# When the next block's weights are split at a change of block

## The chip, the cores and the metric

The kernel runs on one core of a Trainium2 chip. The metric is the device time of one execution in microseconds (us), taken as the median of several. Engines are named as in the profile: PE is TensorE (its weight loads are PEld), DVE is VectorE, ACT is ScalarE, POOL is GpSimd, SP is SyncE, which issues the weight loads.

## The reference, cut to what matters

A sequence of 256 tokens of width 1024 goes through three layers in fp32: one hybrid layer (attention and mLSTM side by side, then an MLP) and two layers of differential attention beside a convolution, each followed by a gated feed-forward part. Around each block stands the same frame:

```
x = x + rms_norm(mixed @ w_out, g_mix_post)        # first layer, "norm"
u = rms_norm(x, g_mlp_pre) @ w_up
x = x + rms_norm(relu(u)**2 @ w_down, g_mlp_post)
...
x = x + (1.0 + gate1) * mixed                      # two later layers, "gate"
h2 = rms_norm_2(x, norm2_g[l]) * (1.0 + scale2) + shift2
f_gate, f_up = jnp.split(h2 @ w_ffn_in[l], 2, axis=-1)
x = x + (1.0 + gate2) * ((jax.nn.silu(f_gate) * f_up) @ w_ffn_out[l])
```

So the last product of a block (w_out, w_down, w_ffn_out) is added to x, the sum is normed row by row, and the normed rows are multiplied by the first weights of the next block.

## The kernel before

**Weights.** All weights stream from HBM once, in pieces called halves here: 128 x 1024 fp32, 512 KB. SP loads each into one of eight buffers `raw` (L192). A half is then split into a high part `whi` on ACT (L202) and the rest `wlo = raw - whi`; three of four rests are made on POOL (L206), the fourth on DVE (L208). A product is three matmuls in the single-pass format: high by high, low by high, high by low. There are nine buffers each of whi and wlo (HB = 9), so a half can be split only when the matmuls of the ninth half before it are done; its raw buffer then takes the next load, in the fixed order of `plan`.

**Order.** The program is written out by hand: each engine runs its instructions in the order of emission. After every half that is used up, `done()` counts it and calls `tick()`, which lets background work go one step and calls `pump()`: it emits splits until nine are made ahead of those used up, or until `rot["cap"]`.

**The change of block.** There are two token blocks, 0 and 1, of 128 rows each. `r_tail` (L397) ends a block: the last halves, 5 (w_out) or 6 (w_down, w_ffn_out), which it has all in hand. It runs them for token block 0 in full, then for token block 1 half by half. While PE is on block 1, the rows of block 0 are finished: added to x, squared and summed (ACT L506, or ACT L553 and DVE L554 first for the norm), the root on POOL (L498, L499), scaled (DVE L511, ACT L512). Then they are turned: eight transposes on PE (L531) into four banks, a gain on DVE (L537) and ACT (L539), and the split into the next block's left operand `hT` (ACT L589, DVE L590). `drain_q(chain)` emits the turning of block 0, ahead of row half CHAIN = 3 of block 1, that is after three of five or six. `done()` stands behind every row half of block 1.

`a2_block` (L321) begins the next block with 6, 7 or 8 halves held (`hold`): it first emits splits until these are made, then runs all for token block 0, with the turning of block 1 put ahead of the last of them (EARLY = 1), and then for block 1. `r_tail` caps the splits at six of them; what is over, the seventh and the eighth, is split at the start of `a2_block`, behind the finishing of block 1 on ACT.

The five changes of block, by their place in the profile, are called first to fifth in this text:

| | from, to | tail halves | held | made before the tail | window, us |
|---|---|---|---|---|---|
| first (norm) | w_out, w_up | 5 | 6 | 1 to 4 | 142 to 163 |
| second (norm) | w_down, w_in of layer 0 | 6 | 8 | 1 to 3 | 333 to 358 |
| third (gate) | w_out, w_ffn_in of layer 0 | 5 | 7 | 1 to 4 | 509 to 528 |
| fourth (gate) | w_ffn_out, w_in of layer 1 | 6 | 8 | 1 to 3 | 702 to 723 |
| fifth (gate) | w_out, w_ffn_in of layer 1 | 5 | 7 | 1 to 4 | 875 to 896 |

At the end of the last block nothing is left to split.

Of the kernel before, what the change touches and what calls it, by code (L numbers as in the profile page):

```python
# [21 lines left out]
NL = 2  # L22
FF1 = 4096
# [7 lines left out]
CAP = 6  # L31
# [6 lines left out]
PRE1, PRE2 = 3, 2  # L38
UPC, GAC = (3, 1), (3, 2)
TAIL = 5  # L40
WARM = 7
EARLY, CHAIN, TWO = 1, 3, 0
SETUP, GATES = 2, 1
TAPS_AT = 2
LOADS = 3
# [12 lines left out]
def tile_hybrid_then_diff(ctx: ExitStack, tc: tile.TileContext, I, out: bass.AP):  # L58
# [121 lines left out]
    state = dict(dma=0, step=0, made=0, taken=0, done=0)  # L180
# [46 lines left out]
    def pump(most=99):  # L227
        while state["step"] < 2 * len(plan) and most > 0:
            most -= 1
            if plan[state["step"] // 2][2] != "a" and (  # L230
                    state["made"] >= min(state["done"] + HB - rot["slack"], rot["cap"])):
                break
            do_step()
# [26 lines left out]
    def done():  # L260
        state["done"] += 1
        tick()

    def tick():
        for d in list(delayed):
            d[0] -= 1
            if d[0] <= 0:
                delayed.remove(d)
                d[1]()
        step_gen(fills)  # L270
        step_gen(fills2)
        if not rot["busy"]:
            step_gen(folds)
        pump()
        for _ in range(rate["bg"]):
            step_gen(bg)

# [116 lines left out]
                mm_tok(acc[t][n], xT, k, t, w, 0, slice(n * 512, n * 512 + 512), start, stop)  # L394
        done()

    def r_tail(tag, srcs, acc, fin, cap, need=None, last=False):  # L397
        rot["slack"] = 0
        pump()
        ws = [take(tag) for _ in srcs]  # L400
        rot["cap"] = state["taken"] + cap
        def mm(t, n, i):
            mm_tok(acc[t][n], srcs[i][0], srcs[i][1], t, ws[i], 0, slice(n * 512, n * 512 + 512),
                   False, i == len(ws) - 1)

        g = fin(0)
        for n in range(2):
            for i in range(len(ws)):
                if need and n == 0:
                    step_gen(fills2)  # L410
                    need(srcs[i][1])
                mm(0, n, i)
            next(g, None)
        chain.append(g)
        rot["busy"] = True
        g = fin(1)
        ahead = range(len(ws) if last else TWO)
        for i in ahead:
            mm(1, 0, i)
        if last:  # L420
            next(g, None)
        for i in range(len(ws)):
            if i == CHAIN:
                drain_q(chain)
            for n in range(1 if i in ahead else 0, 2):
                mm(1, n, i)
            if i == len(ws) - 1:
                if not last:
                    next(g, None)
                next(g, None)  # L430
                pend.append(g)
            done()


    def small(dst, src):
# [135 lines left out]
    def fin(post, t, acc, grow, gc, bc):  # L571
        st = st_tile()
        made = []

        def xn_of():
            if not made:
                made.append(xn_tile())
            return made[0]

        yield from post(t, acc, grow, xn_of, st)  # L580
        scale_x(t, made[0], st)
        yield
        yield from pre_trans(t, made[0], hT, gc, bc)
# [222 lines left out]
    def mod(l, vec, j):  # L806
        assert (l, vec) in made
        return modc[:, l, vec, j:j + 1]
# [57 lines left out]
    def hid_tile():  # L866
        return ab_tile((128, 2, 2, 256), FR)

    def ffn(ng, pre, prefix, up, down_tag, fin, mid=None, last=False):
        hid = {}  # L870
        prefix(hid)
        for g in range(pre, LAG):
            hid[g] = up(g)
        acc = [[acc_tile() for _ in range(2)] for _ in range(2)]
        for g in range(LAG, ng):
            if mid and g == ng - 3:
                mid()
            hid[g] = up(g)
            if g == LAG:
                assert FDEL < 3  # L880
                drain_q(fills)
            h = hid.pop(g - LAG)
            for kk in range(2):
                r_half(down_tag, h, kk, acc, g == LAG and kk == 0, False)
        srcs = [(hid[g], kk) for g in range(ng - LAG, ng) for kk in range(2)]
        r_tail(down_tag, srcs, acc, lambda t: fin(t, acc[t]), CAP, last=last)

    def hid_from_tok(h, full, t):
        ps = ps_tile().rearrange("p (c t) -> p c t", c=4)
# [273 lines left out]
    for k in range(8 - TAIL):  # L1163
# [3 lines left out]
    hT = new_T()  # L1167
    mlp_c = (lambda j: gcol("g_mlp_pre", j), None)
    r_tail("out1", [(mixT, k) for k in range(8 - TAIL, 8)], acc,
           lambda t: fin(post_norm, t, acc[t], gmix, *mlp_c), CAP, need)  # L1170
    gmlp = row_tile(I["g_mlp_post"])

    def prefix1(hid):
# [33 lines left out]
    def to_layer(l, fin):  # L1207
        gc = lambda j: mod(l, 1, j)
        bc = lambda j: mod(l, 0, j)
        return lambda t, acc: fin(t, acc, gc, bc)  # L1210
# [4 lines left out]
            hT = new_T()  # L1215
        yield from fin(post_norm, t, acc, gmlp, gc, bc)

    ffn(FF1 // 256, PRE1, prefix1, up1, "down", to_layer(0, end_mlp))


    for l in range(NL):
# [191 lines left out]
        for k in range(8 - TAIL):  # L1413
# [1 line left out]
        hT = new_T()  # L1415

        r_tail("out2", [(mixT, k) for k in range(8 - TAIL, 8)], acc,
               lambda t: fin(post_gate, t, acc[t], g1, lambda j: mod(l, 4, j), lambda j: mod(l, 3, j)), CAP)
        gfin = row_tile(I["final_g_2"], name="vt") if l == NL - 1 else None
        g2 = []  # L1420

# [40 lines left out]
        def end_all(t, acc):  # L1462
# [7 lines left out]
            yield  # L1470

        ffn(FF2 // 256, PRE2, prefix2, up2, "fo", end_all if l == NL - 1 else to_layer(l + 1, end_layer),
            lambda: g2.append(gate_tile(l, 5)), l == NL - 1)


# [25 lines left out]
```

## Time and profile before

| | |
|---|---|
| median of 3 executions | 1084.35 us (1082.03 to 1085.1) |
| the profiled execution, its own time | 1083.16 us |
| its span, first to last instruction | 1081.4 us |
| PE busy | 1036.0 us, 96% |
| POOL, DVE, ACT busy | 691.5, 647.9, 558.8 us |
| mean granted TensorE clock | 0.985 |

PE is nearly always busy, so the time is PE's work and the few stretches in which it waits or runs at the lower of its two clocks. A row of the timeline below gives the start in us from the span's beginning, the time from start to end, the engine, the line, the operation, output and inputs, shapes, how many instructions were merged, and in brackets the idle time of the engine before it and what ended it.

### The profile page before, as it was taken

The numbers are of one execution on the slowest core, as the hardware profiler recorded it, in microseconds if no ns is written. First come the engines' busy times: TensorE is split into PE (matmuls) and PEld (weight loads), VectorE is DVE, ScalarE is ACT, GpSimd is POOL, SyncE is SP. The second block draws the span as 40 slices with busy tenths as digits, with TensorE's granted clock in tenths as the row PEclk, the third lists the DMA queues.
The fourth block names the chain that finished last, engine by engine and source line by source line (L and its number), as shares of the span: only waits on it lengthen the run. The fifth ranks groups of instructions, "written<-read, shape, count | busy, mean of one in ns | idle before, by whom it ended". The sixth has DMA issues, their size and how long they took to land.

```text
span 1081.4 us, 17255 instructions
## 1 busy us (share of the span) xinstructions
PE 1036.0 (96%) x6459; PEld 917.6 (85%) x6459; DVE 647.9 (60%) x1161; ACT 558.8 (52%) x933; POOL 691.5 (64%) x424
## 2 busy tenths in 40 slices
PE   8879989999998999989999999999999899999997
PEld 6667769899886789988798998888899778999995
DVE  4536556887854497834679797547873554441224
ACT  5745746444455556665643434475676545443441
POOL 2474648566575797846656665859967458566661
PEclk9989999999999999999999999999999999999999
DMA  8554545999974565546499999837635456765631
GB/s 259 169 176 130 192 146 189 345 356 362 329 268 136 167 185 165 187 156 175 132 353 318 332 343 358 299 104 214 186 127 175 137 175 224 258 224 180 198 108 39
DMA packets 169424, 231.84 MB, mean 214 GB/s; under 512 B 10215, under 2 KB 109757, under 8 KB 169339
## 3 DMA queue, kind: packets, MB, share of 16 engines
q1 hardware_dynamic: 169211, 230.71, 65.0%
q8 instruction: 51, 0.84, 0.3%
q14 instruction: 34, 0.28, 0.1%
q0 software_dynamic: 128, 0.02, 0.0%
HBM read 229.64 MB, written 1.06 MB: 213 GB/s over the span
## 4 chain that ended last, share of the span: by engine, by line
PE 75%; POOL 8%; DVE 6%; ACT 6%; issue 3%; DMA 2%; POOLq 0%; SPq 0%; DVEq 0%; ACTq 0%
PE bank L288 17%; PE bank L289 17%; PE bank L290 17%; PE bank L300 12%; POOL wlo L206 6%; PE bank L302 6%; ACT whi L202 2%; DVE bank L762 2%; DVE wlo L208 2%; DMA raw<-in_ada_w_dram 2%; PE bank L840 1%; ACT xn L506 1%; PE bank L860 1%; PE bank L531 1%; PE bank L832 0%
## 5 line engine op out<-in xcount | busy, mean ns | idle before, releaser
L206 POOL TENSOR_TENSOR wlo<-raw,whi 128x1024 fp32r<-128x1024 f32 x255 | 631.5, 2498 | 259.1 <-ACT whi L202 228.4
L202 ACT ACTIVATE whi<-raw 128x1024 fp32r<-128x1024 f32 x332 | 337.4, 1054 | 78.3 <-DMA raw<-in_w_down_dram 30.6
L288 PE MATMUL bank<-T,whi 128*128 128x256 f32 x1072 | 307.7, 287 | 2.3 <-DVE sc L773 2.3
L290 PE MATMUL bank<-T,wlo 128*128 128x256 f32 x1072 | 303.4, 283 | 0.0
L289 PE MATMUL bank<-T,whi 128*128 128x256 f32 x1072 | 303.3, 283 | 0.0
L288 PEld LDWEIGHTS bank<-T,whi 128*128 128x128 f32 x1072 | 205.1, 191 | 6.8 <-issue 3.7
L289 PEld LDWEIGHTS bank<-T,whi 128*128 128x128 f32 x1072 | 205.2, 191 | 1.1
L290 PEld LDWEIGHTS bank<-T,wlo 128*128 128x128 f32 x1072 | 205.1, 191 | 0.0
L300 PE MATMUL bank<-whi,T 128*128 128x512 f32 (+1 forms) x672 | 185.0, 398 | 7.3 <-ACT T L589 4.7
L208 DVE TENSOR_TENSOR wlo<-raw,whi 128x1024 fp32r<-128x1024 f32 x77 | 125.5, 1630 | 100.6 <-ACT whi L202 100.1
L300 PEld LDWEIGHTS bank<-whi,T 128*128 128x128 f32 x672 | 123.9, 192 | 36.6 <-ACT T L589 6.1
L762 DVE SCALAR_TENSOR_TENSOR bank<-raw,cact,bank 128x512 f32<-128x512 f32 x168 | 126.9, 755 | 7.5 <-DMA raw<-in_ada_w_dram 2.1
L288 PE MATMUL bank<-whi,AB 128*128 128x512 f32 x304 | 120.7, 397 | 0.0
L290 PE MATMUL bank<-whi,AB 128*128 128x512 f32 x304 | 120.1, 395 | 0.0
L289 PE MATMUL bank<-wlo,AB 128*128 128x512 f32 x304 | 120.0, 395 | 0.0
L302 PE MATMUL bank<-wlo,T 128*128 128x512 f32 (+1 forms) x336 | 103.8, 393 | 4.0 <-POOL wlo L206 3.0
L1251 DVE SCALAR_TENSOR_TENSOR bank<-cu,cw,bank 128x256 f32<-128x256 f32 x232 | 104.4, 486 | 4.2
L302 PEld LDWEIGHTS bank<-wlo,T 128*128 128x128 f32 x336 | 62.4, 190 | 19.9 <-POOL wlo L206 4.3
L589 ACT ACTIVATE AB<-bank 128x512 fp32r<-128x512 f32 (+1 forms) x49 | 26.0, 537 | 91.3 <-DVE bank L1449 66.2
L290 PEld LDWEIGHTS bank<-whi,AB 128*128 128x128 f32 x304 | 57.3, 188 | 13.4
L288 PEld LDWEIGHTS bank<-whi,AB 128*128 128x128 f32 x304 | 57.4, 189 | 12.0
L289 PEld LDWEIGHTS bank<-wlo,AB 128*128 128x128 f32 x304 | 57.3, 189 | 12.0
(283 smaller groups left out, 1160.5 us busy)
## 6 DMA issues: line engine op xcount, KB each, us to landing
raw<-in_w_in_dram SPq DMA_DIRECT2D x96, 512.0 KB
raw<-in_ada_w_dram SPq DMA_DIRECT2D x96, 512.0 KB
raw<-in_w_ffn_in_dram SPq DMA_DIRECT2D x88, 512.0 KB
raw<-in_w_ffn_out_dram SPq DMA_DIRECT2D x44, 512.0 KB
raw<-in_w_up_dram SPq DMA_DIRECT2D x32, 512.0 KB
raw<-in_w_down_dram SPq DMA_DIRECT2D x32, 512.0 KB
raw<-in_w_out_dram SPq DMA_DIRECT2D x24, 512.0 KB
raw<-in_w_attn_o_dram SPq DMA_DIRECT2D x8, 512.0 KB
```

Source lines behind the costliest of these rows:

```text
L202: A.activation(hi, r, AF.Copy)
L206: G.tensor_sub(lo, r, hi.bitcast(FT))
L208: V.tensor_sub(lo, r, hi.bitcast(FT))
L288: T.matmul(o, lh, rh, start=start, stop=False)
L289: T.matmul(o, lh, rl, start=False, stop=False)
L290: T.matmul(o, ll, rh, start=False, stop=stop)
L300: T.matmul(o, xT[:, a, k0 + kk, ts], w[0][:, kk, cs], start=start and kk == a == 0, stop=False)
L302: T.matmul(o, xT[:, 0, k0 + kk, ts], w[1][:, kk, cs], start=False, stop=stop and kk == kn - 1)
L506: A.activation(halves_of(xn)[n], halves_of(x[t])[n], AF.Square, scale=1.0 / 32, accum_out=st[:, n:n + 1])
L589: A.activation(dst_hi, full, AF.Copy)
L762: V.scalar_tensor_tensor(ada["sum"], r[:, kk, :], cact[:, k:k + 1], ada["sum"], op0=OP.mult, op1=OP.add)
L1251: V.scalar_tensor_tensor(ca[:, j, :] if k == 30 else sums[j], cu[:, j, k:k + 256], cw[:, l * 4 + j, k:k + 1], sums[j], op0=OP.mult, op1=OP ...
```

## The change

The number CHAIN, after how many row halves of token block 1 the rows of block 0 are turned, becomes two: AT_NORM = 4 for the first and second change, AT_GATE = 3 for the others. And the row halves of token block 1 in `r_tail` no longer all call `tick()`: those ahead of the turning only count themselves as done, those behind it let at most two splits be emitted each, and the last is as before.

```
-EARLY, CHAIN, TWO = 1, 3, 0
+EARLY, TWO = 1, 0
+AT_NORM, AT_GATE = 4, 3
...
-    def tick():
+    def tick(most=99):
...
-        pump()
+        pump(most)
...
-    def r_tail(tag, srcs, acc, fin, cap, need=None, last=False):
+    def r_tail(tag, srcs, acc, fin, cap, turn, need=None, last=False):
...
         for i in range(len(ws)):
-            if i == CHAIN:
+            if i == turn:
                 drain_q(chain)
...
-            done()
+            if i < turn:
+                state["done"] += 1
+            elif i < len(ws) - 1:
+                state["done"] += 1
+                tick(2)
+            else:
+                done()
```

`turn` is passed through `ffn` and the three direct calls. On PE only the eight transposes of token block 0 move, and only at the first and second change, behind one more row half. On ACT, DVE and POOL the splits move as the rows show; nothing else on them does, and SP's order is the same. The lines of the changed kernel are numbered one higher up to `r_tail` and seven higher behind it (L202 is L203, L512 is L519).

ACT at the first change of block, before. The row of whi is the fifth and sixth half of the next block; T_1405 is its hT; x_69 and x_70 are the rows of token blocks 0 and 1.

```order
L506 ACTIVATE xn,st<-x_69 128x512 x2
L512 ACTIVATE xn<-x_69,st 128x512
L202 ACTIVATE whi<-raw 128x1024 x2
L539 ACTIVATE bank<-bank,col 128x128 x2
L589 ACTIVATE T_1405<-bank 128x2x128 x2
L539 ACTIVATE bank<-bank,col 128x128 x2
L589 ACTIVATE T_1405<-bank 128x2x128 x2
L553 ACTIVATE xn,st<-bank 128x512 x2
L506 ACTIVATE xn,st<-x_70 128x512 x2
L512 ACTIVATE xn<-x_70,st 128x512
L539 ACTIVATE bank<-bank,col 128x128 x2
```

ACT at the same place, changed:

```order
L513 ACTIVATE xn,st<-x_69 128x512 x2
L519 ACTIVATE xn<-x_69,st 128x512
L546 ACTIVATE bank<-bank,col 128x128 x2
L596 ACTIVATE T_1405<-bank 128x2x128 x2
L546 ACTIVATE bank<-bank,col 128x128 x2
L596 ACTIVATE T_1405<-bank 128x2x128 x2
L560 ACTIVATE xn,st<-bank 128x512 x2
L513 ACTIVATE xn,st<-x_70 128x512 x2
L519 ACTIVATE xn<-x_70,st 128x512
L203 ACTIVATE whi<-raw 128x1024 x2
L546 ACTIVATE bank<-bank,col 128x128 x2
```

The two splits stand behind the turning of token block 0 and also behind the squares and the scaling of block 1, since the only row half behind the turning is the last one, whose call follows the finishing of block 1.

ACT at the second change of block, before (three splits, and then two from `a2_block`):

```order
L512 ACTIVATE xn<-x_69,st 128x512
L202 ACTIVATE whi<-raw 128x1024 x3
L539 ACTIVATE bank<-bank,modc 128x128 x2
L589 ACTIVATE T_3373<-bank 128x2x128 x2
L539 ACTIVATE bank<-bank,modc 128x128 x2
L589 ACTIVATE T_3373<-bank 128x2x128 x2
L553 ACTIVATE xn,st<-bank 128x512 x2
L506 ACTIVATE xn,st<-x_70 128x512 x2
L512 ACTIVATE xn<-x_70,st 128x512
L202 ACTIVATE whi<-raw 128x1024 x2
```

ACT at the second change, changed:

```order
L519 ACTIVATE xn<-x_69,st 128x512
L546 ACTIVATE bank<-bank,modc 128x128 x2
L596 ACTIVATE T_3373<-bank 128x2x128 x2
L546 ACTIVATE bank<-bank,modc 128x128 x2
L596 ACTIVATE T_3373<-bank 128x2x128 x2
L203 ACTIVATE whi<-raw 128x1024 x2
L560 ACTIVATE xn,st<-bank 128x512 x2
L513 ACTIVATE xn,st<-x_70 128x512 x2
L519 ACTIVATE xn<-x_70,st 128x512
L203 ACTIVATE whi<-raw 128x1024 x3
```

Two of the three splits stand behind the turning of block 0, and the third behind the scaling of block 1, together with the seventh and eighth.

ACT at the fourth change of block, before:

```order
L512 ACTIVATE xn<-x_69,st 128x512
L202 ACTIVATE whi<-raw 128x1024 x3
L539 ACTIVATE bank<-bank,modc 128x128 x2
L589 ACTIVATE T_7271<-bank 128x2x128 x2
L539 ACTIVATE bank<-bank,modc 128x128 x2
L589 ACTIVATE T_7271<-bank 128x2x128 x2
L506 ACTIVATE xn,st<-x_70 128x512 x2
L512 ACTIVATE xn<-x_70,st 128x512
L202 ACTIVATE whi<-raw 128x1024 x2
```

ACT at the fourth change, changed:

```order
L519 ACTIVATE xn<-x_69,st 128x512
L546 ACTIVATE bank<-bank,modc 128x128 x2
L596 ACTIVATE T_7271<-bank 128x2x128 x2
L546 ACTIVATE bank<-bank,modc 128x128 x2
L596 ACTIVATE T_7271<-bank 128x2x128 x2
L203 ACTIVATE whi<-raw 128x1024 x3
L513 ACTIVATE xn,st<-x_70 128x512 x2
L519 ACTIVATE xn<-x_70,st 128x512
L203 ACTIVATE whi<-raw 128x1024 x2
```

All three splits (fourth to sixth half) stand between the turning of block 0 and the squares of block 1. On POOL the order there is the same in both: three wlo, then the root of block 1.

## Rows read from the trace of the kernel before

**Rows 1.** The page: memory traffic in 40 slices of the span, 27 us each.

```profile
GB/s 259 169 176 130 192 146 189 345 356 362 329 268 136 167 185 165 187 156 175 132 353 318 332 343 358 299 104 214 186 127 175 137 175 224 258 224 180 198 108 39
```

**Rows 2.** What PE waited for over the whole span: us in total, times, longest us.

```profile
PE bank L300 <- ACT T L589: 4.7, 3, 2.0
PE bank L531 <- DVE xn L511: 3.8, 2, 2.4
PE bank L302 <- POOL wlo L206: 3.0, 3, 1.2
```

**Rows 3.** The timeline at the first change of block, PE, ACT and DVE.

```profile
145.55 1.09 PE L531 MATMUL bank<-ident,xn 128*128 128x128 f32 x8 [2.41 <-DVE xn L511]
...
151.38 2.10 PE L300 MATMUL bank<-whi,T 128*128 128x512 f32 x4 [1.97 <-ACT T L589]
...
160.26 1.04 PE L531 MATMUL bank<-ident,xn 128*128 128x128 f32 x8
...
162.51 1.07 PE L300 MATMUL bank<-whi,T 128*128 128x512 f32 x4
...
145.64 1.99 ACT L202 ACTIVATE whi<-raw 128x1024 fp32r<-128x1024 f32 x2
...
153.36 0.60 ACT L553 ACTIVATE xn<-bank 128x512 f32<-128x512 f32 x1
...
158.95 0.73 ACT L512 ACTIVATE xn<-x,st 128x512 f32<-128x512 f32 x1 [1.07 <-POOL st L499]
...
163.40 0.66 ACT L589 ACTIVATE T<-bank 128x256 fp32r<-128x256 f32 x2 [0.61 <-DVE bank L537]
...
147.66 2.59 DVE L208 TENSOR_TENSOR wlo<-raw,whi 128x1024 fp32r<-128x1024 f32 x1 [2.17 <-ACT whi L202]
```

**Rows 4.** Stretches of the span: length, busy time of PE, PEld, DVE, ACT and POOL (instructions), the granted TensorE clock (1.00 is 2.4 GHz, 0.50 is 1.2 GHz), DMA share and GB/s.

```profile
152.00:153.00 1.00, 1.00 (x3) 0.81 (x4) 0.74 (x3) 0.41 (x2) 0.00 (x0) 0.50 0.84 274
...
155.00:156.00 1.00, 1.00 (x5) 0.83 (x4) 0.67 (x2) 0.00 (x0) 0.58 (x2) 0.92 0.00 0
...
353.00:354.00 1.00, 1.00 (x5) 0.76 (x5) 0.00 (x0) 0.00 (x0) 1.00 (x1) 0.57 0.21 39
...
883.00:885.00 2.00, 1.91 (x7) 1.40 (x8) 1.50 (x4) 1.42 (x6) 0.00 (x0) 1.00 0.93 339
```

**Rows 5.** The timeline at the second change of block, PE, ACT and POOL.

```profile
335.01 1.09 PE L531 MATMUL bank<-ident,xn 128*128 128x128 f32 x8 [1.41 <-DVE xn L511]
...
340.95 1.44 PE L300 MATMUL bank<-whi,T 128*128 128x512 f32 x4 [0.66 <-ACT T L589]
...
350.37 1.21 PE L300 MATMUL bank<-whi,T 128*128 128x512 f32 x4 [0.68 <-ACT whi L202]
...
352.81 0.96 PE L302 MATMUL bank<-wlo,T 128*128 128x512 f32 x2 [1.23 <-POOL wlo L206]
...
357.25 1.07 PE L300 MATMUL bank<-whi,T 128*128 128x512 f32 x4
...
348.64 0.73 ACT L512 ACTIVATE xn<-x,st 128x512 f32<-128x512 f32 x1 [1.07 <-POOL st L499]
...
344.42 0.30 POOL L498 TENSOR_SCALAR st<-st 128x1 f32<-128x1 f32 x1 [2.49 <-ACT xn L553]
...
350.39 4.67 POOL L206 TENSOR_TENSOR wlo<-raw,whi 128x1024 fp32r<-128x1024 f32 x2 [1.64 <-ACT whi L202]
```

**Rows 6.** The timeline at the third change of block, DVE: the split of the fifth half, and the first row of the finishing of token block 1.

```profile
512.79 1.23 DVE L208 TENSOR_TENSOR wlo<-raw,whi 128x1024 fp32r<-128x1024 f32 x1 [1.21 <-ACT whi L202]
...
517.91 0.69 DVE L565 TENSOR_TENSOR bank<-bank,row 128x512 f32<-128x512 f32 x1
```

**Rows 7.** The timeline at the fourth change of block, PE, ACT, POOL and DVE.

```profile
705.39 1.04 PE L531 MATMUL bank<-ident,xn 128*128 128x128 f32 x8
...
719.57 0.73 PE L302 MATMUL bank<-wlo,T 128*128 128x512 f32 x2
...
722.41 1.11 PE L300 MATMUL bank<-whi,T 128*128 128x512 f32 x4
...
705.30 2.94 ACT L202 ACTIVATE whi<-raw 128x1024 fp32r<-128x1024 f32 x3
...
706.41 7.14 POOL L206 TENSOR_TENSOR wlo<-raw,whi 128x1024 fp32r<-128x1024 f32 x3 [1.78 <-ACT whi L202]
715.61 0.30 POOL L498 TENSOR_SCALAR st<-st 128x1 f32<-128x1 f32 x1 [2.05 <-ACT xn L506]
...
718.29 1.23 DVE L208 TENSOR_TENSOR wlo<-raw,whi 128x1024 fp32r<-128x1024 f32 x1 [1.22 <-ACT whi L202]
```

**Rows 8.** The timeline at the fifth change of block, PE, ACT and DVE.

```profile
883.09 1.44 PE L300 MATMUL bank<-whi,T 128*128 128x512 f32 x4 [2.03 <-ACT T L589]
...
894.49 0.73 PE L302 MATMUL bank<-wlo,T 128*128 128x512 f32 x2 [0.87 <-POOL wlo L206]
895.06 1.08 PE L300 MATMUL bank<-whi,T 128*128 128x512 f32 x4
...
877.23 2.00 ACT L202 ACTIVATE whi<-raw 128x1024 fp32r<-128x1024 f32 x2
...
879.26 2.57 DVE L208 TENSOR_TENSOR wlo<-raw,whi 128x1024 fp32r<-128x1024 f32 x1 [2.17 <-ACT whi L202]
...
885.73 0.69 DVE L565 TENSOR_TENSOR bank<-bank,row 128x512 f32<-128x512 f32 x1
```

More of the change, by code (lines that the diff above doesn't have):

```diff
@@ L867, in hid_tile, with ffn @@
         return ab_tile((128, 2, 2, 256), FR)
-    def ffn(ng, pre, prefix, up, down_tag, fin, mid=None, last=False):
+    def ffn(ng, pre, prefix, up, down_tag, fin, turn, mid=None, last=False):
         hid = {}
@@ L885, in ffn @@
         srcs = [(hid[g], kk) for g in range(ng - LAG, ng) for kk in range(2)]
-        r_tail(down_tag, srcs, acc, lambda t: fin(t, acc[t]), CAP, last=last)
+        r_tail(down_tag, srcs, acc, lambda t: fin(t, acc[t]), CAP, turn, last=last)
     def hid_from_tok(h, full, t):
@@ L1169, in tile_hybrid_then_diff @@
     r_tail("out1", [(mixT, k) for k in range(8 - TAIL, 8)], acc,
-           lambda t: fin(post_norm, t, acc[t], gmix, *mlp_c), CAP, need)
+           lambda t: fin(post_norm, t, acc[t], gmix, *mlp_c), CAP, AT_NORM, need)
     gmlp = row_tile(I["g_mlp_post"])
@@ L1216, in end_mlp @@
         yield from fin(post_norm, t, acc, gmlp, gc, bc)
-    ffn(FF1 // 256, PRE1, prefix1, up1, "down", to_layer(0, end_mlp))
+    ffn(FF1 // 256, PRE1, prefix1, up1, "down", to_layer(0, end_mlp), AT_NORM)
     for l in range(NL):
@@ L1417, in tile_hybrid_then_diff @@
         r_tail("out2", [(mixT, k) for k in range(8 - TAIL, 8)], acc,
-               lambda t: fin(post_gate, t, acc[t], g1, lambda j: mod(l, 4, j), lambda j: mod(l, 3, j)), CAP)
+               lambda t: fin(post_gate, t, acc[t], g1, lambda j: mod(l, 4, j), lambda j: mod(l, 3, j)), CAP, AT_GATE)
         gfin = row_tile(I["final_g_2"], name="vt") if l == NL - 1 else None
@@ L1472, in tile_hybrid_then_diff @@
         ffn(FF2 // 256, PRE2, prefix2, up2, "fo", end_all if l == NL - 1 else to_layer(l + 1, end_layer),
-            lambda: g2.append(gate_tile(l, 5)), l == NL - 1)
+            AT_GATE, lambda: g2.append(gate_tile(l, 5)), l == NL - 1)
 _INS = ["x", "positions", "g_mix_pre", "w_in", "b_igate", "b_fgate", "g_mlstm_out", "w_out", "g_mix_post",
```

## The prediction

> **What bounds the kernel now.** I read the busy shares first: PE works 96% of the span, so a change in order can only move the time by what PE waits, or by what it runs at the lower clock. The view of waits comes next. Three of its longest entries belong to the changes of block: for hT (ACT L589) 4.7 us, for the scaled rows (DVE L511) 3.8 us, for wlo from POOL 3.0 us [rows 2]. Then the timeline of each of the five changes, engine by engine, and the granted clock around the long waits. What the reader is to see: at the first change PE waits 2.41 us for the scaled rows of token block 0 before it transposes them, and 1.97 us for hT before the next block begins [rows 3]. At the second change it is 1.41 and 0.66 us, and then 0.68 and 1.23 us more for whi and wlo of later halves [rows 5]. At the third and fourth the next block begins without a wait. At the fifth PE waits 2.03 us for hT, and 0.87 us for the wlo of the seventh half [rows 8].
>
> The cause of the hT waits stands on ACT and DVE: two or three splits sit between the scaling and the turning [rows 3, 5, 8]. At the first change DVE spends 2.59 us on one wlo, beside POOL's, ahead of the gains of hT.
>
> The waits also cost clock: after the first change's waits TensorE was granted 0.50, its 1.2 GHz level, from 152 us until just after 155 us, and again from within 353 to 354 us at the second; behind the fifth's 2.03 us it stayed at 1.00 [rows 4].
>
> **The change, change of block by change of block.** I replay each with durations from before. I measure at one point: the start of token block 1 in the next block, since from there everything hangs on PE and is merely shifted. It was at 162.51, 357.25, 722.41 and 895.06 us at the first, second, fourth and fifth [rows 3, 5, 7, 8]. Three durations recur. From the start of the transposes to the start of the last L589 it is 3.14 us at the first change, with no split ahead (160.26 to 163.40 [rows 3]); for the other changes, where the gain also adds a shift, I put it at 3.4, an estimate, with 0.3 either way. ACT is free 0.55 later. A wlo on POOL begins 1.1 us after its whi begins (705.30 to 706.41) and takes 2.4 (7.14 for three) [rows 7]. A half takes PE 1.37 us, a row half of a tail 1.37 to 1.40.
>
> *First.* One more row half of block 1 now stands ahead of the transposes and fills 1.37 of the 2.41 us. The transposes keep their start, 145.55. One row half is left behind them, so PE is free at 147.9, and hT, with no split ahead, is there: the next block begins at 147.9 instead of 151.38, at full clock, and four halves are done by 153.4. But the fifth and sixth halves are now split behind the scaling of block 1. That chain begins with L553, which goes from 153.36 to 145.55 + 3.14 + 0.55 = 149.2 us; L512 follows 5.6 us later as before (158.95 - 153.36), at 154.8. The whi start at 155.4, and PE can go on at 156.5 (wait 3.1). POOL's wlo is ready at 159.0 (wait 1.5 after 0.9 of work). Then come the transposes of block 1, the sixth half, and the point at 161.6: a gain of 0.9. However, PE has now idled 4.6 of 5.6 us, more than before the clock fell at 152. A low stretch of the length of the old one, begun while it waits or just after, costs up to 1.7. Bounds -0.9 and +0.8; as 2.6 us of PE work (0.45 + 0.8 + 1.37) lie right behind the wait, I take +0.8.
>
> *Second.* The wait of 1.41 is filled, two row halves stay behind the transposes, and the next block begins at 338.7 instead of 340.95. The fourth and fifth whi begin at 335.01 + 3.4 + 0.55 = 339.0, and POOL makes their wlo until 344.8 (4.67 for two [rows 5]). Behind these on POOL stands the root of block 1, which now starts at 344.9 instead of 344.42. With it L512 comes at 349.1 and the sixth whi, now behind it, at 349.7. PE has done five halves by 345.6 and gets the sixth at 350.8: a new wait of 5.2 us. The seventh and eighth wlo end at 356.5 instead of 355.06 (350.39 + 4.67 [rows 5]). At full clock the point is 357.0, that is -0.2. With the low clock, two stretches of it after so long a wait, the sixth half takes 350.8 to 353.5, the seventh ends at 356.2, and with transposes and the eighth the point is 359.2. Bounds -0.2 and +2.5; I take +2.0, near the low clock, as far shorter waits brought it here before.
>
> *Third.* Nothing waited for hT, and two splits go behind it. The first has its wlo on DVE, 1.23 us [rows 6], about 516.8 to 518.0, and DVE was free there: the finishing of block 1 began at 517.91. Shift 0, bounds -0.1 and +0.5 (should POOL's wlo come first and hold DVE for the 2.59 of rows 3, PE's slack of about 1 us ahead of the transposes still hides most of it).
>
> *Fourth.* Nothing waited here either, so there is nothing to win. The three whi go from 705.30 to 705.39 + 3.4 + 0.55 = 709.4, POOL's three wlo end at 709.4 + 1.1 + 7.14 = 717.6, and the root of block 1, third in that queue in both programs, began at 715.61 with POOL idle for 2.05 us before it [rows 7]. That idle time was the cover, and it is gone: the root begins 2.0 later. Behind it hang L512, the seventh whi, and its wlo on DVE (718.29 + 2.0 + 1.23 = 721.5), for which PE's L302 then waits until 721.5 instead of 719.57. Transposes, eighth half and the point follow: +1.8, bounds +1.5 and +2.6 (with some low clock).
>
> *Fifth.* The 2.03 us go: the next block begins at 881.0. The two whi go from 877.23 to about 881.2, the DVE wlo (2.57 beside POOL's) from 879.26 to 883.2 and ends at 885.8. DVE began the finishing of block 1 at 885.73 [rows 8]. So block 1 is not earlier at all, nor is the wlo of the seventh half at 894.5, and PE, two us ahead, waits for the scaled rows and the seventh half instead. The point stays at 895.1: 0, or up to +1.7 if these waits (3.7 of 5.5 us) bring the clock down; behind 2.03 us alone it did not fall [rows 4]. I take +0.4.
>
> *Loads.* The raw buffers of the late splits come free up to 10 to 13 us later, two or three of eight, and SP's queue holds the later loads behind them. The slices with the changes move 104 to 175 GB/s, others up to 362 [rows 1], so I cost this at 0, bounds 0 and +1.
>
> **A rule weighed.** The rows show the clock low after waits of about 2 us (first change) and not after the same wait at the fifth [rows 3, 4, 8]. The Trainium skill, "TensorE: Matmul & The Clock Gate", section "HAM oscillation — how this bites in real kernels", says that it is long gaps, such as a loop's waits for transfers, that put the engine to half rate, and that the next tile then runs cold. Trace and rule differ for the first change's short waits. By the rule alone only the second change's 5.2 us would lower the clock.
>
> **Sum.** 0.8 + 2.0 + 0 + 1.8 + 0.4 = +5.0 on the profiled execution's 1083.16, that is 1088.2. The median of before, 1084.35, is 1.19 above that execution, so I forecast 1089, +0.4%. All low bounds together give +0.3, all high bounds with the loads' +9.1.
>
> **Rivals.**
> - *The clock does not fall, or falls once.* Short waits leave it at 2.4 GHz: -0.9 - 0.2 + 0 + 1.8 + 0 = +0.7, 1085. With the second change low alone +2.9, 1087; that is also what the rule above gives. For it: the fifth change's row. Against it: the first's and second's. 25%.
> - *Faster: the waits vanish and nothing comes late.* The hT waits 1.97 + 0.66 + 2.03, the filled 1.37 + 1.41, and 1.6 of lost clock at the first change make -9: 1075. It needs the late halves to reach PE in time, so that POOL or ACT would have to be some 3 us quicker behind the turning than in the rows; the point from which it decides is the fifth half at the first and the sixth at the second change. Half of it would already be faster. Against it: both queues in the order, and wlo at 2.4 us each. 9%.
> - *Worse: late splits starve the loads and the clock falls at each of the four changes.* All high bounds: 1093. For it: eight raw buffers only; against it: the free bandwidth. 8%.
>
> **How the numbers follow.** Forecast 58%, then 25, 9 and 8. A difference under 0.3% (3.25 us) can't be told from none here, so faster means under 1081.1 and slower over 1087.6. The forecast's own range is 1086.5 to 1091.5; about a tenth of it lies below 1087.6. Slower: 0.9 x 58 + 8 + a little of the first rival, 63%. Same: the first rival and the rest of the forecast, 28%. Faster: 9%. The range that leaves two in ten out reaches over the first rival and most of the worse case: 1083.5 to 1092.5.
>
> **What would show it.** In the profile after: no wait for hT (L596) at the first, second and fifth change; new waits of about 3 us for whi and 1.5 for wlo at the first, 5 us for whi at the second; POOL's root at the fourth straight behind three wlo, and PE waiting there for whi and wlo of the seventh half; at the fifth a wait for xn before the transposes of block 1. The clock at 0.50 near 158 to 162 and 350 to 357 us. If these waits are short, or the clock stays at 1.00, I am wrong on the side of no change.

## The result, and the profile of the changed kernel

| | before | changed |
|---|---|---|
| median of 8 runs | 1084.21 us (1081.34 to 1085.1) | 1089.51 us (1088.32 to 1092.69) |
| ratio of the times, 95% interval | | 1.0055 [1.0042, 1.0067] |
| profiled execution, its span | 1083.16, 1081.4 us | 1089.39, 1087.7 us |
| mean granted clock | 0.985 | 0.981 |

The changed kernel is slower by 5.3 us. The first two lines below are from its page (PE's busy time, and the memory traffic in 40 slices, as in [rows 1]), the others from the view of what PE waited for in all, as in [rows 2] (us in total, times, longest us).

```profile
PE 1038.4 (95%) x6459; PEld 920.4 (85%) x6459; DVE 652.0 (60%) x1161; ACT 559.0 (51%) x933; POOL 690.4 (63%) x424
...
GB/s 255 171 175 128 192 112 216 352 371 343 340 255 112 177 192 164 187 154 174 134 349 318 337 328 362 301 97 211 179 134 175 136 172 221 245 234 178 198 110 39
```

```profile
PE bank L301 <- ACT whi L203: 11.8, 4, 5.2
...
PE bank L303 <- POOL wlo L207: 3.7, 3, 1.3
...
PE bank L538 <- DVE xn L518: 2.7, 2, 1.7
```

PE's wait for hT, 4.7 us in [rows 2], has left the view. In its place stands a wait for whi, 11.8 us in four times. The slices with the first and the fourth change move less (112 where [rows 1] have 146, 97 where they have 104), but the slice behind the first makes it up (216 where they have 189). In the view of what ACT waited for, the entries for loads add up to 72.6 us, before to 77.3. So there is no sign that the loads became the limit.

The **first change**, as in [rows 3]: PE and ACT.

```profile
146.23 1.09 PE L538 MATMUL bank<-ident,xn 128*128 128x128 f32 x8 [1.02 <-DVE xn L518]
...
148.54 1.07 PE L301 MATMUL bank<-whi,T 128*128 128x512 f32 x4
...
157.28 1.19 PE L301 MATMUL bank<-whi,T 128*128 128x512 f32 x4 [2.98 <-ACT whi L203]
159.73 1.22 PE L303 MATMUL bank<-wlo,T 128*128 128x512 f32 x2 [1.25 <-POOL wlo L207]
160.75 1.91 PE L538 MATMUL bank<-ident,xn 128*128 128x128 f32 x8
...
164.00 1.09 PE L301 MATMUL bank<-whi,T 128*128 128x512 f32 x4
...
155.56 0.72 ACT L519 ACTIVATE xn<-x,st 128x512 f32<-128x512 f32 x1 [1.07 <-POOL st L506]
156.19 1.99 ACT L203 ACTIVATE whi<-raw 128x1024 fp32r<-128x1024 f32 x2
```

The next block begins 2.31 us after the transposes (148.54 - 146.23), where it was 5.83 [rows 3]. Then the fifth half is missing: ACT makes its whi only behind the scaling of block 1, and PE waits 2.98 and 1.25 us. The transposes of block 1 take 1.91 us where they took 1.04, which is the low clock.

The **second change**, as in [rows 5].

```profile
336.36 1.10 PE L538 MATMUL bank<-ident,xn 128*128 128x128 f32 x8
...
352.33 2.08 PE L301 MATMUL bank<-whi,T 128*128 128x512 f32 x4 [5.22 <-ACT whi L203]
...
357.50 1.04 PE L538 MATMUL bank<-ident,xn 128*128 128x128 f32 x8
...
359.76 1.09 PE L301 MATMUL bank<-whi,T 128*128 128x512 f32 x4
...
341.54 4.75 POOL L207 TENSOR_TENSOR wlo<-raw,whi 128x1024 fp32r<-128x1024 f32 x2 [5.75 <-ACT whi L203]
346.39 0.30 POOL L505 TENSOR_SCALAR st<-st 128x1 f32<-128x1 f32 x1
...
350.61 0.72 ACT L519 ACTIVATE xn<-x,st 128x512 f32<-128x512 f32 x1 [1.07 <-POOL st L506]
351.24 2.93 ACT L203 ACTIVATE whi<-raw 128x1024 fp32r<-128x1024 f32 x3
```

POOL's root (L505) had 2.49 us of idle time ahead of it [rows 5] and now follows the two wlo with none. The update of x, the squares and the scaling of block 1 (L519) wait for it in turn, and the whi of the sixth half comes behind them on ACT. PE waits 5.22 us for it.

The **fourth change**, as in [rows 7].

```profile
713.57 7.12 POOL L207 TENSOR_TENSOR wlo<-raw,whi 128x1024 fp32r<-128x1024 f32 x3 [5.87 <-ACT whi L203]
720.78 0.30 POOL L505 TENSOR_SCALAR st<-st 128x1 f32<-128x1 f32 x1
...
721.75 0.72 ACT L519 ACTIVATE xn<-x,st 128x512 f32<-128x512 f32 x1 [5.15 <-POOL st L506]
722.38 1.99 ACT L203 ACTIVATE whi<-raw 128x1024 fp32r<-128x1024 f32 x2
...
708.45 1.04 PE L538 MATMUL bank<-ident,xn 128*128 128x128 f32 x8
...
723.48 1.20 PE L301 MATMUL bank<-whi,T 128*128 128x512 f32 x4 [1.65 <-ACT whi L203]
...
727.58 1.10 PE L301 MATMUL bank<-whi,T 128*128 128x512 f32 x4
```

The root stands straight behind three wlo, where POOL had been idle for 2.05 us [rows 7]. The scaling on ACT (L519) waits for it, the whi of the seventh half stands behind the scaling, and PE waits 1.65 us for that whi.

The **fifth change**, as in [rows 8].

```profile
883.46 1.07 PE L538 MATMUL bank<-ident,xn 128*128 128x128 f32 x8
...
887.10 1.07 PE L301 MATMUL bank<-whi,T 128*128 128x512 f32 x4
...
897.14 1.09 PE L538 MATMUL bank<-ident,xn 128*128 128x128 f32 x8 [1.72 <-DVE xn L518]
...
900.77 0.73 PE L303 MATMUL bank<-wlo,T 128*128 128x512 f32 x2 [1.23 <-POOL wlo L207]
901.34 1.09 PE L301 MATMUL bank<-whi,T 128*128 128x512 f32 x4
...
889.52 2.58 DVE L209 TENSOR_TENSOR wlo<-raw,whi 128x1024 fp32r<-128x1024 f32 x1 [1.41 <-ACT whi L203]
892.02 0.69 DVE L572 TENSOR_TENSOR bank<-bank,row 128x512 f32<-128x512 f32 x1
```

The wait for hT is gone (the row at 887.10 has none), but DVE's late wlo holds the finishing of block 1 (L572), and the 2.03 us come back as 1.72 and 1.23.

The clock, as in [rows 4] (length, PE busy, granted clock, DMA share, GB/s):

```profile
159.00:163.00 4.00, 3.27 (x12) 0.57 0.52 153
...
354.00:357.00 3.00, 3.00 (x8) 0.50 0.66 186
...
897.00:901.00 4.00, 2.53 (x13) 1.00 0.09 38
```

To compare runs I use one measure for each change of block: the time from the first transposes of block 0 to token block 1 in the next block, two starts on PE in the timeline. In the changed kernel the first is 164.00 - 146.23 = 17.77.

| | 1st | 2nd | 3rd | 4th | 5th |
|---|---|---|---|---|---|
| before | 16.96 | 22.24 | 15.53 | 17.02 | 17.83 |
| changed | 17.77 | 23.40 | 15.58 | 19.13 | 17.88 |
| difference | +0.81 | +1.16 | +0.05 | +2.11 | +0.05 |

The differences sum to 4.2 us. The two profiled executions are 6.23 us apart. The rest, 2.1 us, lies between the changes: 0.68 ahead of the first, 0.78 and 1.06 around 480 and 850 us, less 0.4 elsewhere. At the two places the clock is low in both profiles, but longer in this one: from 482 to 486 us it was granted 0.50, and 0.89 in the profile before. (Such a stretch at 0.50 is called a low stretch from here on.) This rest is chance and no cost of the change: two runs below, whose code in these stretches is that of the kernel before, also take longer there than its profile does, 1.38 us around 480 (only the fourth change late) and 0.66 around 850 (only the second).

### The profile page after: what moved, and what is told of

Its sections match the earlier page's. It is cut to its first block, busy times and chain, and to the rows that moved or that the text cites. A ratio compares the mean times of both kernels' runs of the same rounds, so it can differ in the third digit from the quotient of the medians.

```text
span 1087.7 us, 17245 instructions
## 1 busy us (share of the span) xinstructions
PE 1038.4 (95%) x6459; PEld 920.4 (85%) x6459; DVE 652.0 (60%) x1161; ACT 559.0 (51%) x933; POOL 690.4 (63%) x424
## 3 DMA queue, kind: packets, MB, share of 16 engines
HBM read 229.64 MB, written 1.06 MB: 212 GB/s over the span
## 4 chain that ended last, share of the span: by engine, by line
PE 71%; POOL 9%; DVE 6%; ACT 5%; issue 5%; DMA 3%; POOLq 0%; SPq 0%; DVEq 0%; ACTq 0%
PE bank L289 17%; PE bank L290 17%; PE bank L291 17%; PE bank L301 10%; POOL wlo L207 7%; PE bank L303 5%; DVE bank L769 2%; ACT whi L203 2%; DVE wlo L209 1%; PE bank L847 1%; DMA raw<-in_ada_w_dram 1%; ACT xn L513 1%; DMA raw<-in_w_ffn_in_dram 1%; POOL st L506 1%; DMA vt<-in_final_g_dram 1%
## 5 line engine op out<-in xcount | busy, mean ns | idle before, releaser
L207 POOL TENSOR_TENSOR wlo<-raw,whi 128x1024 fp32r<-128x1024 f32 x255 | 630.3, 2494 | 278.1 <-ACT whi L203 251.8
L203 ACT ACTIVATE whi<-raw 128x1024 fp32r<-128x1024 f32 x332 | 337.3, 1054 | 74.3 <-DMA raw<-in_w_down_dram 29.7
L301 PE MATMUL bank<-whi,T 128*128 128x512 f32 (+1 forms) x672 | 184.1, 398 | 12.2 <-ACT whi L203 11.8
L209 DVE TENSOR_TENSOR wlo<-raw,whi 128x1024 fp32r<-128x1024 f32 x77 | 129.2, 1678 | 97.3 <-ACT whi L203 96.7
```

The costliest lines, as they stand in the source:

```text
L203: A.activation(hi, r, AF.Copy)
L207: G.tensor_sub(lo, r, hi.bitcast(FT))
L209: V.tensor_sub(lo, r, hi.bitcast(FT))
L301: T.matmul(o, xT[:, a, k0 + kk, ts], w[0][:, kk, cs], start=start and kk == a == 0, stop=False)
```

## Experiments

The experiments hold the change in two tables with an entry for each change of block (the sixth is the last tail, behind which no block follows): `TURN`, the row halves ahead of the turning, and `LATE`, 1 where the splits are held back and 0 where `done()` is called as before. The changed kernel is `(4, 4, 3, 3, 3, 3)` and all 1; the kernel before is all 3 and all 0. Line numbers are some higher than in the changed kernel: whi is L205 to L207, wlo L209 to L215.

Three theories stand at the start. A: late halves and the root of block 1 queue in order on POOL and ACT, and PE waits for what stands last. B: the new place of the transposes costs the time. C: the late splits free the raw buffers late and starve the loads.

**One or two changes alone.** The fourth:

```diff
-TURN, LATE = (4, 4, 3, 3, 3, 3), (1, 1, 1, 1, 1, 1)
+TURN, LATE = (3, 3, 3, 3, 3, 3), (0, 0, 0, 1, 0, 0)
```

> Late splits at the fourth change of block alone (w_ffn_out to w_in of layer 1), all else as before. Theory A (late halves and the root of block 1 queue in order on POOL and ACT): the start of token block 1 moves +2.0 us against the start of the transposes of block 0 (17.0 us in before, 19.1 in the changed kernel), POOL's root straight behind three wlo, total +2 us (+0.2%). Theory B (the place of the turning costs): +0, since the turning does not move here. Theory C (late splits free raw buffers late and starve the loads, wherever they stand): waits of ACT for loads grow behind this change, total +1 to +2 but spread over the later layer, not at this point.

Measured: 19.14 at the fourth change, +2.12, and the whole 1.0013 [1.0003, 1.0023]. So Theory A's size stands, and the cost needs no other change. This run also has an unchanged first and second change, with 16.23 and 20.73 us instead of 16.96 and 22.24. Its PE and its clock at the second change:

```profile
352.20 1.20 PE L303 MATMUL bank<-whi,T 128*128 128x512 f32 x4 [0.69 <-ACT whi L205]
354.65 0.74 PE L305 MATMUL bank<-wlo,T 128*128 128x512 f32 x2 [1.25 <-POOL wlo L209]
```

```profile
350.00:356.00 6.00, 4.06 (x21) 1.00 0.07 11
```

The same waits as in [rows 5] (0.68 and 1.23), the same code, and no low clock. In the kernel before it fell there [rows 4], and that was worth 22.24 - 20.73 = 1.5 us. So a low stretch behind waits of this size is a matter of the single execution.

The third and fifth:

```diff
+TURN, LATE = (3, 3, 3, 3, 3, 3), (0, 0, 1, 0, 1, 0)
```

> Late splits at the third and fifth change alone. Theory A: PE no longer waits for hT at the fifth (2.03 us in before) but waits as much for the rows of block 1 and the seventh half: 0 at both points, total 0 (-0.5 to +0.7). Theory B: 0. Theory C: +1 to +2, as two of the four late changes are there.

Measured: 15.58 and 17.88, +0.05 each, the whole 1.0000 [0.9986, 1.0014]. As expected; Theory C, under which two late splits at each of the two changes should cost 1 to 2 us, has nothing for it, here or in ACT's waits for loads above.

The turning moved behind a fourth row half, with no split held back:

```diff
+TURN, LATE = (4, 4, 3, 3, 3, 3), (0, 0, 0, 0, 0, 0)
```

> The turning one row half later at the first and second change, splits as in before. Theory A: PE waits less at the transposes and more for hT (DVE's gain still waits for its wlo), the next block begins when it did: 0 at both points, total 0. Theory B: +2 us, since half of the change is here. Theory C: 0.

Measured: 16.97 at the first (with a low stretch) and 20.73 at the second, the whole 1.0004 [0.9992, 1.0016]. PE waits less for the scaled rows and more for hT (3.3 us at the first), as expected. The place of the transposes costs nothing that these show, and Theory B's +2 us is outside the interval.

The first alone, and the second alone:

```diff
+TURN, LATE = (4, 3, 3, 3, 3, 3), (1, 0, 0, 0, 0, 0)
```

> Only the first change of block as in the changed kernel (four row halves ahead of the transposes, no split before block 0 is turned); the other four as before. Theory A (the late whi and wlo, queued on ACT and POOL behind the turning, take the place of the wait for hT): waits of about 3 us for whi and 1.3 for wlo before the second transposes, from the first transposes to token block 1 in the next block 17.8 us (17.76 in the changed kernel) where an unchanged first change took 16.23 to 16.97; the whole +0.8 to +1.5 us, ratio 1.001. Theory D (the rise in the changed kernel was chance of the clock): 16.3 without a low stretch and no difference in the whole. Rival of the faster side: the waits 1.97 and 2.41 gone, -2 us.

```diff
+TURN, LATE = (3, 4, 3, 3, 3, 3), (0, 1, 0, 0, 0, 0)
```

> Only the second change of block as in the changed kernel; the other four as before. Theory A: POOL's root of block 1 straight behind two wlo, the sixth whi behind it, PE waits about 5.2 us for it; from the first transposes to token block 1 in the next block 23.4 us (23.40 in the changed kernel), against 20.73 where an unchanged second change meets no low clock and 22.25 where it does; the whole +1.2 to +2.7 us, ratio 1.001 to 1.0025. Theory D (the 5.2 us wait is old waits added up, and only the clock differs): 20.7 to 22.3 and no difference in the whole.

Measured: 17.66 at the first, with the waits of 3.0 and 1.2 us, and 23.65 at the second, with the 5.2 us. The sizes at the changes are Theory A's. The whole is 1.0009 [0.9994, 1.0023] and 1.0007 [0.9991, 1.0022]: each interval holds both the expected and no difference, so the times alone would not have told.

**All splits behind the turning, at three row halves everywhere.**

```diff
+TURN, LATE = (3, 3, 3, 3, 3, 3), (1, 1, 1, 1, 1, 1)
```

> The changed kernel with AT_NORM = 3: all five changes late, but at the first and second the splits now stand between the turning of block 0 and the finishing of block 1. Theory A: first change -1.4 us against before (PE waits for the rows of block 1, not for late whi), second +0.4 (seventh wlo behind a root that starts 0.5 later), third 0, fourth +2.0, fifth 0: about +1 us in all against before, 3 us less than the changed kernel at these points. Theory B: -2 or more against the changed kernel, all of it at the transposes of block 0. Theory C: no better than the changed kernel.

Measured: 15.99 at the first, -0.96 (-0.24 against the 16.23 above), but 24.05 at the second, +1.80; the whole 1.0038 [1.0023, 1.0052], some 4 us where about 1 was expected. The second was the miss. Its POOL and DVE:

```profile
340.91 5.76 POOL L209 TENSOR_TENSOR wlo<-raw,whi 128x1024 fp32r<-128x1024 f32 x2 [5.76 <-ACT whi L205]
346.77 0.30 POOL L511 TENSOR_SCALAR st<-st 128x1 f32<-128x1 f32 x1
...
342.76 1.65 DVE L211 TENSOR_TENSOR wlo<-raw,whi 128x1024 fp32r<-128x1024 f32 x1 [2.36 <-ACT whi L205]
```

With three late splits DVE takes one wlo between POOL's two, and POOL's pair lasts 5.76 instead of 4.75 us. The root follows 11.04 us after the transposes, against 10.03 in the changed kernel. So the queue ahead of the root is longer still, and the chain behind the root with it.

**What keeps the fifth change from winning.** Both late wlo go to POOL there (`ON_POOL`), so that DVE has nothing ahead of the finishing of block 1.

```diff
-        if rot["n"] >= 1.0:
+        if due or state.get("force"):
             G.tensor_sub(lo, r, hi.bitcast(FT))
...
+TURN, LATE = (3, 3, 3, 3, 3, 3), (0, 0, 0, 0, 1, 0)
+ON_POOL = (0, 0, 0, 0, 1, 0)
```

> Only the fifth change: no split until block 0 is turned, then two, as in the changed kernel, but both late wlo on POOL (in the changed kernel one of them is DVE's, 2.58 us, ahead of the finishing of token block 1); all else as before. Theory A (what keeps the fifth change from winning is that DVE's late wlo holds the finishing of block 1, so that PE waits 1.72 us for xn and 1.23 for the wlo of the seventh half): DVE's finishing begins about 888 instead of 892 on the changed kernel's clock, the wait for xn goes, about 1.3 us stay for the last wlo, and from the first transposes to token block 1 it takes about 15.8 us instead of 17.88 (bounds 14.9 and 16.6); the whole -1.3 to -2.9 us, ratio 0.998. Theory B (POOL with its root is the bound, the DVE split doesn't matter): 17.8, no difference.

```profile
883.86 4.76 POOL L212 TENSOR_TENSOR wlo<-raw,whi 128x1024 fp32r<-128x1024 f32 x2 [5.82 <-ACT whi L206]
888.72 0.30 POOL L516 TENSOR_SCALAR st<-st 128x1 f32<-128x1 f32 x1
...
883.27 0.69 DVE L583 TENSOR_TENSOR bank<-bank,row 128x512 f32<-128x512 f32 x1
...
890.53 1.03 PE L549 MATMUL bank<-ident,xn 128*128 128x128 f32 x8
...
893.87 0.73 PE L308 MATMUL bank<-wlo,T 128*128 128x512 f32 x2 [1.25 <-POOL wlo L212]
```

Measured: 15.73 instead of 17.83, and the whole 0.9982 [0.9968, 0.9996]. DVE's finishing begins 4.6 us after the transposes (883.27 - 878.71; 8.6 in the changed kernel), the wait for xn is gone, and 1.25 us for the last wlo stay. So what held the fifth change was DVE's late wlo, as Theory A has it. Here too the root stands straight behind POOL's two wlo, but PE has six halves to do before it needs xn, and xn is ready by then.

With the first change added, at three row halves:

```diff
+TURN, LATE = (3, 3, 3, 3, 3, 3), (1, 0, 0, 0, 1, 0)
+ON_POOL = (0, 0, 0, 0, 1, 0)
```

> Transposes after three row halves as before; the splits held until block 0 is turned at the first and at the fifth change alone, at the fifth with both late wlo on POOL; second, third and fourth change as before. If the effects of the single runs add up: first change 16.0 us from the first transposes to token block 1 in the next block (15.99 in the run with all at three row halves), that is 0 to -0.96 beside an unchanged first change (16.23 to 16.97), and the fifth 15.8 (-2); the whole -2 to -3 us, ratio 0.997 to 0.998. Rival: each wait won is taken up again by the next one or by the clock, and no difference.

Measured: 15.95 and 15.74, as expected; 1081.13 us, ratio 0.9978 [0.9964, 0.9991]. It beats both kernels, the one before by 2.6 us of the medians beside it (1083.75), the changed one, by the ratios of each to the kernel before, by some 8. What the first change adds to the fifth's 0.9982 is too small for the times to show.

**Is it the root's place on POOL?** First the fourth change alone, with the root of block 1 on DVE:

```diff
+ROOT = (0, 0, 0, 1, 0, 0)
...
+            E.tensor_scalar(q.bitcast(I32), s.bitcast(I32), 1, None, op0=OP.arith_shift_right)
+            E.tensor_scalar(y.bitcast(I32), q.bitcast(I32), -1, 0x5F375A80, op0=OP.mult, op1=OP.add)
+            for i in range(3):
+                E.scalar_tensor_tensor(q, y, s, y, op0=OP.mult, op1=OP.mult)
+                E.tensor_scalar(q, q, -0.5, 1.5, op0=OP.mult, op1=OP.add)
+                E.tensor_tensor(o if i == 2 else y, q, y, op=OP.mult)
```

> The fourth change alone as in the changed kernel (three splits behind the turning), but the inverse root of token block 1 is made on DVE, by a first guess from the bits and three Newton steps (11 small instructions, put at some 0.15 us each from DVE's 128x1 rows, 1.7 us) instead of two on POOL. All else as before. Theory A (the +2.12 us is the root's place behind three wlo in POOL's queue): DVE has the root some 1.8 us after ACT's last square, instead of 5.2 us with POOL, the seventh whi comes 3 us earlier, PE's wait of 1.68 us for it goes, and from the first transposes to token block 1 in the next block it takes 17.0 to 17.3 us, as in the kernel before (17.02); no difference in the whole. Theory B (what is late is the turning's place itself, or the third wlo): 19.1 as with the root on POOL (19.14), the whole +2.

```profile
712.23 7.13 POOL L213 TENSOR_TENSOR wlo<-raw,whi 128x1024 fp32r<-128x1024 f32 x3 [5.87 <-ACT whi L207]
...
715.91 1.10 DVE L526 SCALAR_TENSOR_TENSOR st<-st 128x1 f32<-128x1 f32 x1
717.05 0.15 DVE L527 TENSOR_SCALAR st<-st 128x1 f32<-128x1 f32 x1
717.24 2.13 DVE L528 TENSOR_TENSOR st<-st 128x1 f32<-128x1 f32 x1
719.41 0.22 DVE L526 SCALAR_TENSOR_TENSOR st<-st 128x1 f32<-128x1 f32 x1
...
719.85 0.16 DVE L528 TENSOR_TENSOR st<-st 128x1 f32<-128x1 f32 x1
```

A miss, for both theories: 21.07, part of it a low stretch from 724 us, and the whole 1.0047 [1.003, 1.0064]. The root left POOL's queue and was later still: xn is scaled from 720.68, 13.58 us after the transposes (720.68 - 707.10), where the changed kernel has 13.30 (721.75 - 708.45). The rows show why: an instruction on one number a partition took 1.10 and 2.13 us on DVE, each until POOL's current wlo ended, and 0.22 and 0.16 once the three were done at 719.36. Those with one tensor from SBUF took 0.15 to 0.21 us throughout. So POOL's wlo stop DVE too, where it reads two tensors from SBUF. The Trainium skill, "SBUF — State Buffer", section "SBUF: two separate sides", says this: the pair of ports that the two engines share is locked for a whole instruction. The 2.13 us agree. At the fourth change the root's place is thus not tested by itself: that it makes the 2.1 us is read from the rows, where the root, L519, the whi and PE all move by that much.

Then the second change alone, with two instructions on DVE in the place of the root's two on POOL (this kernel leaves out the power, so its numbers are not the reference's):

```diff
+            E.tensor_scalar(o, st[:, 0:1], 0.0, 1.0, op0=OP.mult, op1=OP.add)
...
+ROOT = (0, 1, 0, 0, 0, 0)
```

> The second change alone as in the changed kernel, but the two inverse roots of token block 1 there leave POOL: DVE makes two instructions of the same size in their place, and the power is left out (the root is taken as 1), so that only the place in the queue differs. All else as before. Theory A (PE's 5.2 us for the sixth whi come from the root behind two wlo on POOL, and from L519 and the whi behind the root on ACT): the root is made about 2.7 us earlier, at 344.6 instead of 347.3 on the changed kernel's clock, the whi about 3 us earlier, PE waits about 2.2 us, and from the first transposes to token block 1 in the next block it takes 19.2 to 20.8 us, against 23.4 to 23.65 with the root on POOL and 20.7 to 22.25 in the kernel before; the whole -1.5 to +0 us. Theory B (ACT's own order, or the raw halves from memory, makes the whi late): the 5.2 us stay, 23.4 to 23.7, the whole +1.

```profile
340.90 4.76 POOL L213 TENSOR_TENSOR wlo<-raw,whi 128x1024 fp32r<-128x1024 f32 x2 [5.76 <-ACT whi L207]
...
343.82 0.15 DVE L522 TENSOR_SCALAR st<-st 128x1 f32<-128x1 f32 x1
344.01 2.85 DVE L582 SCALAR_TENSOR_TENSOR x<-sc,st,x 128x512 f32<-128x512 f32 x2
...
349.87 1.19 PE L307 MATMUL bank<-whi,T 128*128 128x512 f32 x4 [3.41 <-ACT whi L207]
```

Measured: PE's wait falls from 5.22 to 3.41 us, the measure to 21.30 (with a low stretch), the whole 0.9997 [0.9984, 1.0010]. Theory B's 23.4 is excluded. But a wait of 2.2 us and a measure of 19.2 to 20.8 were expected. Most of the gap is the row L582: x is updated from two tensors in SBUF and takes 2.85 us instead of 1.41, as it waits for POOL's wlo to end. So taking the root out of POOL's queue gives 1.8 of the 5.22 us, and the same two wlo on POOL hold back another 1.4 through DVE. The 2 us that are left no run takes apart; the whi of the sixth half still stands behind the whole finishing of block 1 on ACT.

**Do the parts make the whole?** The changed kernel again (no edit but the tables), and its first, second and fourth change together:

> The changed kernel once more, to see which part of its +5.3 us is fixed. The five changes: +0.8, +1.2 to +2.7, 0, +2.1 and 0 (17.7, 23.4 to 23.7, 15.6, 19.1 and 17.9 us from the first transposes to token block 1). Theory A (the pieces add up, and the 2.1 us outside the changes in the first profile are mostly its clock): the whole +3 to +5 us, ratio 1.003 to 1.0045, and outside the changes another sum than +2.1. Theory E (late splits cost something outside the changes as well, so that the whole is more than its pieces): +5 to +7 us, ratio 1.0045 to 1.0065, and again about 2 us outside the changes, at the same places.

```diff
+TURN, LATE = (4, 4, 3, 3, 3, 3), (1, 1, 0, 1, 0, 0)
```

> The first, second and fourth change as in the changed kernel, the third and fifth as before: the three to which the traces give all of the cost, 0.7 to 1.1, 1.2 to 1.4 and 2.1 us (17.7 to 18.0, 23.4 to 23.7 and 19.1 us from the first transposes to token block 1), the third 15.5 and the fifth 17.8 to 18.2. Theory A (the pieces add up): together +4.0 to +4.6 us, ratio 1.0037 to 1.0042, though the single runs gave 1.0009, 1.0007 and 1.0013, 1.0029 together. Theory E (the third and fifth change, or all five together, cost something elsewhere): the ratio stays near 1.003, clearly under the changed kernel's 1.0055 and 1.0064.

Measured: the changed kernel again 1.0064 [1.0046, 1.0081], the three together 1.0057 [1.0037, 1.0077]. In the traces the first, second and fourth take 18.04, 23.54 and 19.14 us in the one and 18.03, 23.56 and 19.14 in the other, +4.5 both times. So the three that cost make the loss, and the third and fifth none that the intervals, some 2 us wide to either side, can show; Theory E falls as far as it puts a cost on these two. Outside the changes the first of the two profiles has +4.4 us instead of +2.1, most of it (2.92) ahead of the first change. That part is chance: the run with only the fourth change late, whose code up to there is that of the kernel before, has +2.55.

Both times came out above Theory A's ranges, though. What these left out is that the one profile of the kernel before is a draw. The measure over all profiles in which a change of block is as in the kernel before, and over those in which it is as in the changed kernel:

| | 1st | 2nd | 3rd | 4th | 5th |
|---|---|---|---|---|---|
| as before, lowest to highest | 16.21 to 17.02 | 20.70 to 22.27 | 15.52 to 15.54 | 17.00 to 17.02 | 17.82 to 18.21 |
| as before, mean | 16.45 | 21.36 | 15.53 | 17.01 | 18.01 |
| as changed, mean | 17.88 | 23.53 | 15.58 | 19.14 | 17.88 |
| difference | +1.4 | +2.2 | 0 | +2.1 | -0.1 |

Against these means, of 4 to 10 profiles each, the five changes cost 5.6 us, a ratio of 1.0052, and the three 5.7, 1.0053. Both lie in the intervals measured. The single changes would come to 1.0013, 1.0020 and 1.0020, which their intervals hold too, the second and the fourth just so. That the three single runs sum to 1.0029 only is within their width, and no run says more.

## Why the prediction came out as it did

It said 1089.0 us and the median is 1089.5. By its steps:

- *First, +0.8: measured +0.81.* Each link came as replayed: the next block 2.3 us after the transposes (2.31), L519 at 9.25 (9.33), waits of 3.1 and 1.5 us (2.98 and 1.25), and the low clock, 0.57 from 159 to 163 us, where 158 to 162 was said. But the term holds against a profile in which the old waits, too, had brought a low stretch that cost time. Against an unchanged first change without that cost (16.23) the change costs 1.5, and against the mean 1.4. The replay was right and its base was not.
- *Second, +2.0: measured +1.16.* The wait was sized at 5.2 us and is 5.22; the sixth and seventh half at low clock end at 21.2 us after the transposes as replayed (357.50 - 336.36 = 21.14). The mis-sized step is the last, "with transposes and the eighth the point is 359.2": it gave them 3.0 us, at a partly low clock, and they took 2.26, since the clock was back by 357.5. And the base was a draw as well: 20.73 is the unchanged second change at full clock. Against the mean the change costs 2.2, so a replay 0.8 too late (24.2 against 23.4) and a base 0.9 too high came out near the truth together, which is luck.
- *Third, 0: +0.05.*
- *Fourth, +1.8: +2.11.* Root behind three wlo, whi, DVE's wlo, PE, as replayed; everything moved by the root's 2.11 (12.33 after the transposes, before 10.22), and the 0.2 that I took off were not there. What the prediction lacked is that POOL's wlo also stop DVE's instructions with two tensors from SBUF. Here that changed nothing; in a repair it decides.
- *Fifth, +0.4: +0.05.* No earlier finishing behind DVE's wlo, as argued, and the waits of 1.72 and 1.23 us left the clock at 1.00, in all four profiles with this change. The row of [rows 4] on which I leaned, no low clock behind 2.03 us, was a draw: in five of the eight profiles with the unchanged fifth change the clock fell to 0.50 there, and the measure is 18.00 to 18.21 instead of 17.82.
- *Loads, 0:* the traffic rows and ACT's waits for loads agree.

The sum was 5.0, the five terms from the two profiles give 4.2, those against the means 5.6, and the medians differ by 5.3. So the mechanism was right at each change, and the forecast that it gave is near; that it is within 1 us owes something to errors against each other, since every term was set against one profile of a kernel whose own changes of block vary by some 1.5 us with the clock.

The rivals: the clock did fall at two of the changes, so 1085 to 1087 did not come, nor did the waits vanish. The rule of the Trainium skill, "TensorE: Matmul & The Clock Gate", section "HAM oscillation — how this bites in real kernels", would have had the clock low at the second change alone. It was also low behind 2.98 and 1.25 us at the first, in every run with that change. Behind the short waits of the unchanged second change it was low in some runs (22.24) and not in others (20.73), so for these neither the rule nor my reading of one profile gives a price.

## What to carry to other kernels

Work that is pushed behind a critical step does not vanish from its queue: find what stands next in that queue and how much idle time it has ahead of it, for that is the cover, and what is beyond it comes back as a new wait. Held-back work pays where two things hold, as at the fifth change with both wlo on POOL: the engine at the end of the chain has other work meanwhile (six halves on PE), and the held-back work goes to an engine that the next step doesn't need first. Before a low stretch of the clock is counted as a cost of a wait, look at a second profile of the same code, and take the base of a forecast from more than one.

## What was not expected of the hardware

- POOL's 128x1024 subtractions hold DVE instructions that read two tensors from SBUF until the running one ends, down to one number a partition: 2.13 instead of 0.16 us, and 2.85 instead of 1.41 for the update of x.
- Equal waits on equal code (0.68 and 1.23 us) came with the granted clock at 1.00 in one execution and at 0.50 in another, 1.5 us apart. Behind the fifth change's 2.03 us it was 1.00 in three profiles and 0.50 in five.
